# A hybrid encoder layer on one core: operand buffers, copy priority, DMA queues and mixer pacing in the last block

## The chip, the core and the metric

The kernel runs on one core of a Trainium2 chip. The core has five engines that run side by side, each with its own instruction queue in program order: TensorE (PE in the profile, with PEld for its weight loads), VectorE (DVE), ScalarE (ACT), GpSimd (POOL) and SyncE (SP). Data moves between DRAM and the on-chip memory by DMA; a DMA is issued by SP (queue SPq) or by POOL (queue POOLq), and an issue that must wait stands in front of all that was put behind it on the same engine. The metric is the device time of one execution in microseconds (us), lower is better.

## What is computed

One layer of a streaming trunk over 2,064 prompt rows and 64 sample rows of width 1024, in float32:

```python
def _trunk(x, states, segs, p):
    for l in range(DEPTH):                       # DEPTH = 1
        m, ns = _mixer(_rmsnorm(x, p['norm1_w'][l]), l, *st, segs, p)   # input projection, three head groups (SSD, RWKV-7, HGRN2), w_out
        x = x + m
        x = x + _swiglu(_rmsnorm(x, p['norm2_w'][l]), p['w_gate'][l], p['w_up'][l], p['w_down'][l])
    return _rmsnorm(x, p['final_norm_w']), ...

def _swiglu(h, wg, wu, wd):
    return (jax.nn.silu(h @ wg) * (h @ wu)) @ wd
```

The feed-forward width is 2816, that is 22 column blocks of 128. The mixers are causal recurrences in chunks; beside the rows, their final states are returned.

## The kernel before

Each float32 operand of a large product is split into a high and a low part (ACT copies the high part, `AF.Copy` to float32r; DVE, or POOL in the early phase, subtracts for the low one), and a product is three matmuls: high by high, high by low, low by high. A weight block w with both parts is 512 KB; five buffers hold such blocks (WB = 5), and three hold raw 256 KB blocks that are still to be split (tile `raw`, RB = 3).

**The early phase.** Rows are 17 tiles of 128. Nine are worked off in three early blocks of three tiles (class `Ffn`: output projection `out`, gate and up columns and down products in `ffn`, last down products and final norm in `rest`). `early()` runs these blocks as the dense main stream of PE work; the mixers run beside them as side streams ("rw" and "hs", for the RWKV-7 and HGRN2 groups). A planner merges both: each dense step advances a clock `now` by its cost in matmul columns, and a stream may take its next step when its own time, which grows by its step's cost times a scale, is not past `now`. The scales are RWX and HSX (L42): larger scales put more dense work between two steps of a mixer. The last early block does SWITCH of the 22 column blocks of its `ffn` under the planner together with the mixers; then what is left of the mixers is drained, the operands `ya` of the last block (outputs of the mixers) are loaded (24 loads by SP, 256 KB each), and the rest of the `ffn` runs.

**The last block** has the remaining eight tiles and multiplies in blocks of two by two with seven products instead of eight. It runs in this order:

- `first_half(j)`: output projection (key "wo") and norm, which leaves the hidden rows as operands (`op`, `ya`, split at L1412/L1413).
- Pairs i = 0 to 10: gate and up columns, seven products each (`columns`). A bank of sums is copied by ACT from PSUM to a tile `c` (`copy`, L1553). The weight sums t1 to t4 of a pair are made from raw loads (`lraw`, L1534), but for the first PRE = 3 pairs they were made ahead and lie in DRAM (`raw`, L1360). At the end of a pair, `finish` applies the gate (L1604, L1605), forms four sums (L1608 to L1611) and POOL writes the seven results to DRAM (tiles `ma..`, `ms..`, L1614).
- After each pair, `t_sums` makes the sums of two w_down blocks (`wd0` to `wd10`): SP loads four quarters (L1315), DVE adds, POOL stores (L1320).
- The down products (`tokens_first` with key "wd"): seven products, each over 11 k-blocks. Operands come back from DRAM in groups of four k-blocks (`m_group`: load `mraw`, L1638, up to 1 MB; split to `op` by ACT L1412 and DVE L1413). `mraw` has two buffers in a pool l2 that is opened when the pool lp of the pairs is closed and lies in lp's memory. POOL loads the residual rows `acc` (L1656). Results are added to `acc` (L1375).
- `final_norm`: two squares with row sums on ACT (L1133), the sum and the power (L1134, POOL L230), two scalings on DVE (L1138), two 256 KB stores by POOL (L1139).

The order of instructions on each engine is made by a scheduler at build time; memory that is reused makes the new owner wait for the readers and DMAs of the old one.

Of the kernel before, what the change touches and what calls it, by code (L numbers as in the profile page):

```python
# [13 lines left out]
AF = mybir.ActivationFunctionType  # L14
# [5 lines left out]
P = 128  # L20
# [3 lines left out]
NFF = DFF // P  # L24
# [14 lines left out]
GKS = 1  # L39
GLO = 3  # L40
URB = 6
RWX, HSX, HSD = 1.05, 1.0, 6.0  # L42
COL = 1 / 2360
AHEAD = 4
KOUT = [8, 9, 10, 11, 0, 1, 2, 3, 4, 5, 6, 7]
# [1 line left out]
DSTEP = (-1, 2, 6, 9)  # L47
FW = 3
NH = 4
SWITCH = 14  # L50
PRE = 3
TAIL = 4
CW = 384
# [25 lines left out]
def body(tc, A, O, blocks=None, supers=None, dbg=None):  # L79
    nc = tc.nc  # L80
    V, S, G, T = nc.vector, nc.scalar, nc.gpsimd, nc.tensor
# [5 lines left out]
    def pool(st, name, bufs=1, **kw):  # L87
        return st.enter_context(tc.tile_pool(name=name, bufs=bufs, **kw))
# [7 lines left out]
    def mk(p, shape, dt=F32, tag=None, bufs=None):  # L96
        uid[0] += 1
        kw = {} if bufs is None else {"bufs": bufs}
        return p.tile(list(shape), dt, tag=tag, name=f"{tag}_{uid[0]}", **kw)
# [1024 lines left out]
                    nc.sync.dma_start(dbg["y"][k, t], yscr[k][t])  # L1124


    def final_norm(p, xt, t, n, fw):

        s2 = mk(p, [P, 2], tag="s2", bufs=2)
        ss = mk(p, [P, 1], tag="ss", bufs=2)  # L1130
        for hf in range(2):
            dump = mk(p, [P, 512], tag="w2k", bufs=4)
            S.activation(dump[:n], xt[:, hf * 512:hf * 512 + 512], AF.Square, accum_out=s2[:n, hf:hf + 1])  # L1133
        V.tensor_tensor(ss[:n], s2[:n, 0:1], s2[:n, 1:2], ADD)  # L1134
        rs = inv_rms(p, ss, n, 1, 1.0 / D, EPS)
        for hf in range(2):
            cs = slice(hf * 512, hf * 512 + 512)
            V.scalar_tensor_tensor(xt[:, cs], xt[:, cs], rs[:n], fw[:n, cs], MUL, MUL)  # L1138
            G.dma_start(O["y_prompt"][(t - 1) * P:t * P, cs] if t else O["y_sample"][:, cs], xt[:, cs])  # L1139

    class Ffn:

# [132 lines left out]

        def final(self, i, fw):
            t, n = self.tiles[i], self.lens[i]
            final_norm(self.fp, self.acc[:n, i, :], t, n, fw)

    if supers:  # L1280
        stE, st = ExitStack(), ExitStack()
# [3 lines left out]
        def early():  # L1285
            drain(ALLY(EARLY[0]))
            fs[0].start()
            for i, f in enumerate(fs):
# [10 lines left out]
                else:  # L1299
                    yield from f.ffn(0, SWITCH)  # L1300

# [6 lines left out]

        tdram = {}

        def t_sums(key, q):

            def ld(n):
                r = mk(ring, [P, 512], tag="raw", bufs=RB)
                nc.sync.dma_start(r, q[n])  # L1315
                return r

            def st(n, r):
                d = tdram[key, n] = dram.tile([P, 512], F32, tag=f"{key}{n}", name=f"{key}{n}")
                G.dma_start(d, r)  # L1320

            a, b = ld(3), ld(1)
            V.tensor_tensor(a, a, b, SUB)
            st("t3", a)
            c_ = ld(0)
            V.tensor_tensor(b, b, c_, SUB)
            st("t1", b)
            V.tensor_tensor(c_, a, c_, ADD)
            st("t2", c_)
            d_ = ld(2)  # L1330
            V.tensor_tensor(d_, d_, c_, SUB)
            st("t4", d_)

        def quarters(key, kk):
            if key in ("w_gate", "w_up"):
                return [A[key][2 * kk + f][:, h * 512:h * 512 + 512] for h in range(2) for f in range(2)]
            if key == "wo":
                k = kk // 2 * 4 + kk % 2
                return [A["w_out"][d, k + 2 * h] for h in range(2) for d in range(2)]
            return [A["w_down"][(2 * kk + h) * P:(2 * kk + h + 1) * P, d * 512:d * 512 + 512] for h in range(2) for d in range(2)]  # L1340

        def prep_sums():
            for key, kks in (("wo", (4, 5, 0, 1, 2, 3)), ("w_gate", range(PRE)), ("w_up", range(PRE))):
                for kk in kks:
                    t_sums(f"{key}{kk}", quarters(key, kk))
                    yield 35.0

        def parts(raw):
# [62 lines left out]
        def to_parts(hi, lo, src):  # L1411
            S.activation(hi, src, AF.Copy)  # L1412
            V.tensor_tensor(lo, src, hi.bitcast(F32), SUB)  # L1413

        tile_of = lambda h, j: LATE[h][j]
# [23 lines left out]
        acc = [[mk(lo_, [P, D], tag=f"acc{h}{j}", bufs=1) for j in range(NH)] for h in (1, 0)][::-1]  # L1439
# [84 lines left out]
        msc = {(n, g): dram.tile([P, 4, 512], F32, tag=f"m{n}{g}", name=f"m{n}{g}") for n, *_ in PRODS for g in range(3)}  # L1524
        stF = ExitStack()

        def columns(key, i):

            q = dict(zip(("b11", "b12", "b21", "b22"), quarters(key, i)))
            raw = {}  # L1530
            if i >= PRE:
                for n in ("b22", "b12", "b11", "b21"):
                    raw[n] = mk(lp, [P, 512], tag="lraw", bufs=8)
                    nc.sync.dma_start(raw[n], q[n])  # L1534
                b11, b12, b21, b22 = (raw[n] for n in q)
                V.tensor_tensor(b22, b22, b12, SUB)
                V.tensor_tensor(b12, b12, b11, SUB)
                V.tensor_tensor(b11, b22, b11, ADD)
                V.tensor_tensor(b21, b21, b11, SUB)
                raw = {"t3": b22, "t1": b12, "t2": b11, "t4": b21}  # L1540

            def prod(ps, a, b, first=True):
                hi, lo = parts(raw[b]) if b in raw else b_part(key, i, b)
                ah, al = hop[a]
                for k in range(4):
                    wh, wl = (x[:, k * P:(k + 1) * P] for x in (hi, lo))
                    mm(ps, wh, ah[:, k], first and k == 0, False, not first)
                    mm(ps, wh, al[:, k], False, False, not first)
                    mm(ps, wl, ah[:, k], False, k == 3, not first)

            def copy(tag, ps, bufs):
                r = mk(lp, [P, 512], tag=tag, bufs=bufs)
                S.activation(r, ps, AF.Copy)  # L1553
                return r

            add = lambda r, ps: V.tensor_tensor(r, ps, r, ADD)
            pre = i < PRE
            x = xbank()
            prod(x, "s1", "t1")
            c22 = copy("c22", x, 6)  # L1560
            yield
            y = xbank() if pre else ybank()
            prod(y, "a22", "t4")
            c21 = copy("c21", y, 6)
            yield
            z = ybank()
            prod(z, "a11", "b11")
            c11 = copy("c11", z, 4)
            yield
            y = ybank()  # L1570
            prod(y, "a12", "b21")
            add(c11, y)
            yield
            prod(z, "s2", "t2", False)
            c12 = copy("c12", z, 4)
            yield
            if pre:
                add(c12, c22)
                x = xbank()
            prod(x, "s4", "b22", pre)  # L1580
            add(c12, x)
            yield
            prod(z, "s3", "t3", False)
            add(c21, z)
            add(c22, z)
            return c11, c12, c21, c22
# [29 lines left out]
        for j in range(NH):  # L1616
            first_half(j)
        stO.close()
        lp = pool(stF, "lp", reuse_waits="tile")
        pairs = [Pair(i) for i in range(PRE)]  # L1620
        for p_ in pairs:
# [2 lines left out]
        for i in range(NFF // 2):  # L1624
            if i >= PRE:
                pairs.append(Pair(i))
            pairs[i].finish()
            t_sums(f"wd{i}", quarters("wd", i))
        stF.close()


        l2 = pool(st, "l2", reuse_waits="tile")
        mraw = lambda: mk(l2, [P, 4, 512], tag="mraw", bufs=2)

        def m_group(name, kks):
            n = len(kks)
            raw = mraw()
            nc.sync.dma_start(raw[:, :n], msc[name, kks[0] // 4][:, :n])  # L1638
            hi, lo = op_tile()
            to_parts(hi[:, :n], lo[:, :n], raw[:, :n])  # L1640
            return [(hi[:, i], lo[:, i]) for i in range(n)]

        def finish(h, j):
            final_norm(l2, acc[h][j], tile_of(h, j), P, fw)

        def rows_done(a):
            if a == "s1":
                for j in range(NH):
                    finish(1, j)

        acc = [[mk(l2, [P, D], tag=f"acc{h}{j}", bufs=1) for j in range(NH)] for h in range(2)]
        fw = mk(l2, [P, D], tag="nw", bufs=1)
        ahead_ = m_group("a11", range(4))
        for h in range(2):
            for j in range(NH):
                G.dma_start(acc[h][j], xs2[h][j])  # L1656
        G.dma_start(fw, A["fw"].partition_broadcast(P))
        tokens_first("wd", list(range(NFF // 2)), 4, lambda n, kks: ahead_ if (n, kks[0]) == ("a11", 0) else m_group(n, kks), acc, rows_done, lambda prepare: None, lambda j: finish(0, j))
        st.close()
    else:  # L1660
        drain(ALLY(range(last_tile + 1)))
# [110 lines left out]
```

## Time and profile before

| What | Value |
|---|---|
| Three runs | 3590.32, 3579.01, 3581.46 us; median 3581.46 |
| The profiled execution | 3584.01 us; span in the trace 3582.0, so 2.0 lie around it |
| PE busy | 3376.5 us (94%) |
| DVE, ACT, POOL busy | 2200.1 (61%), 1237.6 (35%), 727.5 (20%) |
| Last matmul ends, span ends | 3567.3, 3582.0 us |

PE is the engine with the most work, so time can be saved where PE stands idle, where it runs below its full clock, and behind its last matmul. In the views quoted below a row of the timeline is: start, duration, engine, line, operation, out<-in, shapes, count, and in brackets the idle time before it with what ended that time. A row of the windows is: window, its length, then busy time and count for PE, PEld, DVE, ACT and POOL, the granted TensorE clock (1.00 is full), the share of the DMA engines' time that was busy, and GB/s. A row of the waits is: what waited, for what, total us, times, the longest.

### The profile page before, as it was taken

The numbers are of one execution on the slowest core, as the hardware profiler recorded it, in microseconds if no ns is written. First come the engines' busy times: TensorE is split into PE (matmuls) and PEld (weight loads), VectorE is DVE, ScalarE is ACT, GpSimd is POOL, SyncE is SP. The second block draws the span as 40 slices with busy tenths as digits, with TensorE's granted clock in tenths as the row PEclk, the third lists the DMA queues.
The fourth block names the chain that finished last, engine by engine and source line by source line (L and its number), as shares of the span: only waits on it lengthen the run. The fifth ranks groups of instructions, "written<-read, shape, count | busy, mean of one in ns | idle before, by whom it ended". The sixth has DMA issues, their size and how long they took to land.

```text
span 3582.0 us, 60919 instructions
## 1 busy us (share of the span) xinstructions
PE 3376.5 (94%) x22588; PEld 2950.8 (82%) x22588; DVE 2200.1 (61%) x4940; ACT 1237.6 (35%) x2618; POOL 727.5 (20%) x1022
## 2 busy tenths in 40 slices
PE   7999999999999998889898999999999989999798
PEld 7998789889799996778776899879888868788686
DVE  3358455557766676787777776767425655654453
ACT  4445333344343444344342222223102442223241
POOL 3325202102111112344442211110101002210001
PEclk9999999999999999899999999999999989999899
DMA  9776865555765668788899997676787458865755
GB/s 321 233 224 220 285 213 177 155 161 177 242 218 175 202 195 290 270 282 307 306 309 328 312 330 253 226 266 229 229 276 263 158 162 282 282 217 174 274 180 207
DMA packets 430497, 860.40 MB, mean 240 GB/s; under 512 B 112096, under 2 KB 211944, under 8 KB 426360
## 3 DMA queue, kind: packets, MB, share of 16 engines
q1 hardware_dynamic: 405752, 775.23, 65.7%
q0 software_dynamic: 24448, 81.28, 6.1%
q8 instruction: 178, 2.92, 0.3%
q14 instruction: 119, 0.97, 0.1%
HBM read 603.81 MB, written 252.54 MB: 239 GB/s over the span
## 4 chain that ended last, share of the span: by engine, by line
PE 29%; issue 13%; DMA 6%; DVE 5%; POOL 3%; ACT 1%; SPq 1%; POOLq 0%; DVEq 0%; ACTq 0%
PE g L111 21%; PE d L111 4%; DMA w<-w 2%; PE h L111 2%; PE c L111 1%; DMA raw<-in_w_down 1%; DMA raw<-in_w_gate 1%; POOL w L222 1%; DMA raw<-in_w_up 1%; POOL ms L1614 1%; POOL ma L1614 0%; DMA raw<-in_w_out 0%; DVE acc L1274 0%; DVE tp L640 0%; DVE Xp L641 0%
## 5 line engine op out<-in xcount | busy, mean ns | idle before, releaser
L111 PE MATMUL g<-hhi,w 128*128 128x384 f32 (+3 forms) x3312 | 832.7, 329 | 15.0 <-ACT stage L368 4.7
L111 PEld LDWEIGHTS g<-hhi,w 128*128 128x128 f32 (+1 forms) x3312 | 579.2, 188 | 30.2 <-ACT stage L368 5.1
L111 PE MATMUL g<-h2hi,w 128*128 128x384 f32 (+1 forms) x2112 | 544.4, 334 | 12.6 <-ACT w L220 5.3
L111 PE MATMUL g<-hlo,w 128*128 128x384 f32 (+3 forms) x1680 | 549.1, 327 | 0.0
L111 PEld LDWEIGHTS g<-h2hi,w 128*128 128x128 f32 x2112 | 375.9, 190 | 23.3 <-ACT w L220 7.9
L111 PE MATMUL g<-h2lo,w 128*128 128x384 f32 (+1 forms) x1056 | 349.6, 331 | 0.8 <-DVE h2lo L255 0.8
L111 PEld LDWEIGHTS g<-hlo,w 128*128 128x128 f32 (+1 forms) x1680 | 313.5, 187 | 5.6
L222 POOL TENSOR_TENSOR w<-raw,w 128x512 fp32r<-128x512 f32 x180 | 247.7, 1378 | 336.9 <-ACT w L220 284.4
L111 PE MATMUL g<-w,mhi 128*128 128x512 f32 x792 | 264.3, 411 | 18.3 <-ACT w L220 6.1
L220 ACT ACTIVATE w<-raw 128x512 fp32r<-128x512 f32 x240 | 149.8, 629 | 197.8 <-PE g L111 52.6
L111 PE MATMUL g<-w,op 128*128 128x512 f32 x816 | 197.0, 401 | 22.1 <-ACT op L1412 22.1
L111 PEld LDWEIGHTS g<-w,op 128*128 128x128 f32 x816 | 155.5, 191 | 61.1 <-ACT op L1412 23.0
L111 PEld LDWEIGHTS g<-h2lo,w 128*128 128x128 f32 x1056 | 200.1, 189 | 4.1 <-DVE h2lo L255 1.4
L111 PEld LDWEIGHTS g<-w,mhi 128*128 128x128 f32 x792 | 150.0, 194 | 54.4 <-ACT w L220 7.0
L111 PE MATMUL g<-w,hhi 128*128 128x512 f32 (+1 forms) x544 | 179.8, 411 | 11.4 <-DMA w<-w 7.4
L111 PE MATMUL d<-op,w 128*128 128x512 f32 x720 | 170.4, 395 | 8.2 <-DMA w<-w 8.2
L111 PEld LDWEIGHTS d<-op,w 128*128 128x128 f32 x720 | 136.0, 189 | 39.7 <-issue 9.8
L1274 DVE TENSOR_TENSOR acc<-g,acc 128x512 f32<-128x512 f32 (+1 forms) x198 | 133.0, 684 | 52.1 <-PE g L111 51.8
L640 DVE TENSOR_TENSOR tp<-Xp,b4k 128x60 f32<-128x60 f32 (+24 forms) x527 | 126.1, 239 | 62.8 <-DMA b4k<-psc 50.4
L111 PE MATMUL g<-w,mlo 128*128 128x512 f32 x396 | 159.8, 404 | 0.0
L111 PE MATMUL d<-w,op 128*128 128x512 f32 x612 | 144.1, 395 | 0.0
L111 PEld LDWEIGHTS d<-w,op 128*128 128x128 f32 x612 | 114.7, 187 | 28.1
(435 smaller groups left out, 6214.8 us busy)
## 6 DMA issues: line engine op xcount, KB each, us to landing
w<-w SPq DMA_DIRECT2D x893, 512.0 KB, 4.4
raw<-in_w_down SPq DMA_DIRECT2D x88, 256.0 KB, 4.2
hin<-hg SPq DMA_DIRECT2D x16, 1280.0 KB, 6.0
rin<-rw SPq DMA_DIRECT2D x16, 896.0 KB, 6.0
raw<-in_w_gate SPq DMA_DIRECT2D x56, 256.0 KB, 4.4
raw<-in_w_up SPq DMA_DIRECT2D x56, 256.0 KB, 4.8
hg<-stage SPq DMA_DIRECT2D x64, 192.0 KB, 3.0
raw<-in_w_out SPq DMA_DIRECT2D x48, 256.0 KB, 5.1
```

The costliest lines, as they stand in the source:

```text
L111: return T.matmul(out, lhsT, rhs, start=start, stop=stop, skip_group_check=more)
L220: S.activation(hi, raw, AF.Copy)
L222: (G if units[0] % 4 < GLO else V).tensor_tensor(lo, raw, wt[:, 0], SUB)
L640: V.tensor_tensor(tv, _bc(Xp[:, 0:m, q], 2, w), _bc(Up[:, q, q + 1:32], 1, m), MUL)
L1274: V.tensor_tensor(self.acc[:n, i, cs], ps[:n], self.acc[:n, i, cs], ADD)
L1614: G.dma_start(msc[n, g][:, k, :], r)
```

## The change

Six edits:

1. The loads of gated rows (`m_group`) get a pool of their own, `lm`, opened before the pairs on the other side of the memory, with three buffers of two k-blocks instead of two buffers of four; a group is loaded and split in two halves. The first group is asked for ahead of the `acc` tiles.
2. Copies of a bank in `columns` get high priority in the scheduler for the first three pairs.
3. The loads of `t_sums` go through a queue that the caller names: POOL's for the w_down sums, SP's as before for the sums made ahead.
4. RWX 1.05 to 1.08, HSX 1.0 to 1.03, SWITCH 14 to 18.
5. `final_norm` can take a tile in which the first square's sum already lies; for the first half of the last block's rows these squares are issued after the product "a12", the last that adds to the first 512 columns.
6. The stores of these rows go through SP's queue.

```diff
-RWX, HSX, HSD = 1.05, 1.0, 6.0
+RWX, HSX, HSD = 1.08, 1.03, 6.0
-SWITCH = 14
+SWITCH = 18
...
+    def squares(p, xt, n, hf, s2):
+        dump = mk(p, [P, 512], tag="w2k", bufs=4)
+        S.activation(dump[:n], xt[:, hf * 512:hf * 512 + 512], AF.Square, accum_out=s2[:n, hf:hf + 1])
+
+    def final_norm(p, xt, t, n, fw, queue, s2=None):
...
-        for hf in range(2):
-            dump = mk(p, [P, 512], tag="w2k", bufs=4)
-            S.activation(dump[:n], xt[:, hf * 512:hf * 512 + 512], AF.Square, accum_out=s2[:n, hf:hf + 1])
+        if s2 is None:
+            s2 = mk(p, [P, 2], tag="s2", bufs=2)
+            squares(p, xt, n, 0, s2)
+        squares(p, xt, n, 1, s2)
...
-            G.dma_start(O["y_prompt"][(t - 1) * P:t * P, cs] if t else O["y_sample"][:, cs], xt[:, cs])
+            queue.dma_start(O["y_prompt"][(t - 1) * P:t * P, cs] if t else O["y_sample"][:, cs], xt[:, cs])
...
-        def t_sums(key, q):
+        def t_sums(key, q, queue):
...
-                nc.sync.dma_start(r, q[n])
+                queue.dma_start(r, q[n])
...
-                S.activation(r, ps, AF.Copy)
+                with tc.high_priority() if i < PRE else ExitStack():
+                    S.activation(r, ps, AF.Copy)
...
+        lm = pool(st, "lm", side="right", reuse_waits="tile")
         lp = pool(stF, "lp", reuse_waits="tile")
...
-            t_sums(f"wd{i}", quarters("wd", i))
+            t_sums(f"wd{i}", quarters("wd", i), G)
...
-        mraw = lambda: mk(l2, [P, 4, 512], tag="mraw", bufs=2)
...
-            raw = mraw()
-            nc.sync.dma_start(raw[:, :n], msc[name, kks[0] // 4][:, :n])
             hi, lo = op_tile()
-            to_parts(hi[:, :n], lo[:, :n], raw[:, :n])
+            for a in range(0, n, 2):
+                w = min(2, n - a)
+                raw = mk(lm, [P, 2, 512], tag="mraw", bufs=3)
+                nc.sync.dma_start(raw[:, :w], msc[name, kks[0] // 4][:, a:a + w])
+                to_parts(hi[:, a:a + w], lo[:, a:a + w], raw[:, :w])
...
+        ahead_ = m_group("a11", range(4))
+        sq = [mk(l2, [P, 2], tag="sq", bufs=NH) for _ in range(NH)]
 
         def rows_done(a):
-            if a == "s1":
-                for j in range(NH):
-                    finish(1, j)
+            for j in range(NH):
+                if a == "s1":
+                    final_norm(l2, acc[1][j], tile_of(1, j), P, fw, G)
+                elif a == "a12":
+                    squares(l2, acc[0][j], P, 0, sq[j])
...
+                     lambda j: final_norm(l2, acc[0][j], tile_of(0, j), P, fw, nc.sync, sq[j]))
```

How this moves instructions is shown at three places. The first is SP's queue where the pairs end and the down products begin. Before, `w125` to `w173` are the first five w_down blocks that need no sums, and the first loads of gated rows (`mraw<-ma110`, four k-blocks each) stand behind them:

```order
L216 DMA w_4848_33511<-w230_20537 128x1024
L216 DMA w_4849_33526<-w232_20587 128x1024
L216 DMA w_4871_33645<-w125_16970 128x1024
L216 DMA w_4872_33659<-w137_17385 128x1024
L216 DMA w_4873_33673<-w149_17719 128x1024
L216 DMA w_4874_33687<-w161_18198 128x1024
L216 DMA w_4877_33706<-w173_18600 128x1024
L1638 DMA mraw_4865_33627<-ma110_30194 128x2048
L1638 DMA mraw_4875_33701<-ma111_30195 128x2048
```

In the change, the same stretch of SP's queue:

```order
L216 DMA w_4848_33514<-w230_20381 128x1024
L216 DMA w_4849_33529<-w232_20482 128x1024
L1645 DMA mraw_4889_33782<-ma112_30196 128x512
L1645 DMA mraw_4898_33837<-ms30_30197 128x1024
L216 DMA w_4876_33656<-w125_16884 128x1024
L216 DMA w_4877_33670<-w137_17262 128x1024
L1645 DMA mraw_4899_33841<-ms30_30197 128x1024
L1645 DMA mraw_4909_33914<-ms31_30198 128x1024
L216 DMA w_4878_33684<-w149_17639 128x1024
L216 DMA w_4879_33698<-w161_18022 128x1024
```

The loads of `ma110`, and of the first half of `ma111`, no longer stand here at all: they went up into the pairs. Its last group (`ma112`, which holds pair 10) and the first group of the next product (`ms30`) now stand ahead of `w125`.

The second place is SP's queue around pairs 2 to 4 (`w134`, `w136` belong to pair 2, `w141` to pair 3). Before, loads for the w_down sums (`raw<-in_w_down`) stand between the loads of gate columns (`lraw`) and of weight blocks:

```order
L216 DMA w_4511_31130<-w136_17334 128x1024
L1315 DMA raw_4517_31204<-in_w_down 128x512
L1315 DMA raw_4518_31209<-in_w_down 128x512
L1534 DMA lraw_4562_31521<-in_w_gate 128x512
L1315 DMA raw_4519_31217<-in_w_down 128x512
L1534 DMA lraw_4563_31523<-in_w_gate 128x512
L1315 DMA raw_4558_31501<-in_w_down 128x512
L1534 DMA lraw_4564_31525<-in_w_gate 128x512
L1315 DMA raw_4559_31503<-in_w_down 128x512
L1315 DMA raw_4560_31508<-in_w_down 128x512
L1534 DMA lraw_4565_31527<-in_w_gate 128x512
L216 DMA w_4541_31319<-w141_17491 128x1024
```

In the change SP has only the loads that PE's own work needs, but for one load of gated rows a little later (`ma110`, pairs 2 and 3):

```order
L216 DMA w_4511_31133<-w136_17231 128x1024
L1538 DMA lraw_4562_31524<-in_w_gate 128x512
L1538 DMA lraw_4563_31526<-in_w_gate 128x512
L1538 DMA lraw_4564_31528<-in_w_gate 128x512
L1538 DMA lraw_4565_31530<-in_w_gate 128x512
L216 DMA w_4541_31322<-w141_17416 128x1024
```

```order
L1538 DMA lraw_4572_31560<-in_w_up 128x512
L1645 DMA mraw_4858_33626<-ma110_30194 128x1024
L1538 DMA lraw_4604_31823<-in_w_gate 128x512
L1538 DMA lraw_4605_31825<-in_w_gate 128x512
L1538 DMA lraw_4606_31827<-in_w_gate 128x512
```

The loads that are gone from here stand in POOL's queue now, between the stores of the same sums and the writes of the pairs' results (`wd3`, `wd4` are the sums of two w_down blocks, `ma110` is a result of pair 3):

```order
L1324 DMA wd3t4_31522<-raw_4561_31519 128x512
L1319 DMA raw_4601_31805<-in_w_down 128x512
L1319 DMA raw_4602_31810<-in_w_down 128x512
L1619 DMA ma110_30194<-c11_4542_31336 128x512
L1324 DMA wd4t3_31808<-raw_4600_31803 128x512
L1324 DMA wd4t1_31813<-raw_4601_31805 128x512
L1324 DMA wd4t2_31816<-raw_4602_31810 128x512
L1319 DMA raw_4603_31818<-in_w_down 128x512
```

The third place is ACT's queue where `first_half` ends and the pairs begin: the last splits of hidden rows (`op<-hraw`) and the first four copies of banks. Before:

```order
L1412 ACTIVATE op_4369_30193<-hraw0_4220_29260 128x4x128
L1412 ACTIVATE op_4367_30191<-hraw1_4221_29261 128x4x128
L1412 ACTIVATE op_4369_30193<-hraw0_4220_29260 128x4x128
L1553 ACTIVATE c22_4391_30355<-g_4388_30337 128x512
L1553 ACTIVATE c22_4395_30375<-g_4392_30357 128x512
L1553 ACTIVATE c21_4399_30395<-g_4396_30377 128x512
L1553 ACTIVATE c21_4403_30415<-g_4400_30397 128x512
```

In the change:

```order
L1416 ACTIVATE op_4369_30193<-hraw0_4220_29260 128x4x128
L1416 ACTIVATE op_4367_30191<-hraw1_4221_29261 128x4x128
L1416 ACTIVATE op_4369_30193<-hraw0_4220_29260 128x4x128
L1558 ACTIVATE c22_4391_30358<-g_4388_30340 128x512
L1558 ACTIVATE c21_4399_30398<-g_4396_30380 128x512
L1558 ACTIVATE c22_4395_30378<-g_4392_30360 128x512
L1558 ACTIVATE c21_4403_30418<-g_4400_30400 128x512
```

The copies stand behind the last split as before; the second and third of them have changed places.

More of the change, by code (lines that the diff above doesn't have):

```diff
@@ L1124, in body @@
                     nc.sync.dma_start(dbg["y"][k, t], yscr[k][t])
-    def final_norm(p, xt, t, n, fw):
-        s2 = mk(p, [P, 2], tag="s2", bufs=2)
+    def squares(p, xt, n, hf, s2):
+        dump = mk(p, [P, 512], tag="w2k", bufs=4)
+        S.activation(dump[:n], xt[:, hf * 512:hf * 512 + 512], AF.Square, accum_out=s2[:n, hf:hf + 1])
+    def final_norm(p, xt, t, n, fw, queue, s2=None):
         ss = mk(p, [P, 1], tag="ss", bufs=2)
-        for hf in range(2):
-            dump = mk(p, [P, 512], tag="w2k", bufs=4)
-            S.activation(dump[:n], xt[:, hf * 512:hf * 512 + 512], AF.Square, accum_out=s2[:n, hf:hf + 1])
+        if s2 is None:
+            s2 = mk(p, [P, 2], tag="s2", bufs=2)
+            squares(p, xt, n, 0, s2)
+        squares(p, xt, n, 1, s2)
         V.tensor_tensor(ss[:n], s2[:n, 0:1], s2[:n, 1:2], ADD)
@@ L1277, in final @@
             t, n = self.tiles[i], self.lens[i]
-            final_norm(self.fp, self.acc[:n, i, :], t, n, fw)
+            final_norm(self.fp, self.acc[:n, i, :], t, n, fw, G)
     if supers:
@@ L1344, in prep_sums @@
                 for kk in kks:
-                    t_sums(f"{key}{kk}", quarters(key, kk))
+                    t_sums(f"{key}{kk}", quarters(key, kk), nc.sync)
                     yield 35.0
@@ L1627, in body @@
             pairs[i].finish()
-            t_sums(f"wd{i}", quarters("wd", i))
+            t_sums(f"wd{i}", quarters("wd", i), G)
         stF.close()
         l2 = pool(st, "l2", reuse_waits="tile")
-        mraw = lambda: mk(l2, [P, 4, 512], tag="mraw", bufs=2)
         def m_group(name, kks):
             n = len(kks)
-            raw = mraw()
-            nc.sync.dma_start(raw[:, :n], msc[name, kks[0] // 4][:, :n])
             hi, lo = op_tile()
-            to_parts(hi[:, :n], lo[:, :n], raw[:, :n])
+            for a in range(0, n, 2):
[3 more added lines that the diff above has]
+                to_parts(hi[:, a:a + w], lo[:, a:a + w], raw[:, :w])
             return [(hi[:, i], lo[:, i]) for i in range(n)]
-        def finish(h, j):
-            final_norm(l2, acc[h][j], tile_of(h, j), P, fw)
+        ahead_ = m_group("a11", range(4))
+        sq = [mk(l2, [P, 2], tag="sq", bufs=NH) for _ in range(NH)]
         def rows_done(a):
-            if a == "s1":
-                for j in range(NH):
-                    finish(1, j)
+            for j in range(NH):
[3 more added lines that the diff above has]
+                    squares(l2, acc[0][j], P, 0, sq[j])
         acc = [[mk(l2, [P, D], tag=f"acc{h}{j}", bufs=1) for j in range(NH)] for h in range(2)]
         fw = mk(l2, [P, D], tag="nw", bufs=1)
-        ahead_ = m_group("a11", range(4))
         for h in range(2):
@@ L1657, in body @@
         G.dma_start(fw, A["fw"].partition_broadcast(P))
-        tokens_first("wd", list(range(NFF // 2)), 4, lambda n, kks: ahead_ if (n, kks[0]) == ("a11", 0) else m_group(n, kks), acc, rows_done, lambda prepare: None, lambda j: finish(0, j))
+        tokens_first("wd", list(range(NFF // 2)), 4, lambda n, kks: ahead_ if (n, kks[0]) == ("a11", 0) else m_group(n, kks), acc, rows_done, lambda prepare: None,
+                     lambda j: final_norm(l2, acc[0][j], tile_of(0, j), P, fw, nc.sync, sq[j]))
         st.close()
```

## The prediction

> **What bounds the kernel now.** I read the page's busy shares first, then the windows over the stretches that the change touches, then the timeline of PE, SP, ACT and POOL at the gaps.
>
> ```profile
> PE 3376.5 (94%) x22588; PEld 2950.8 (82%) x22588; DVE 2200.1 (61%) x4940; ACT 1237.6 (35%) x2618; POOL 727.5 (20%) x1022
> ```
> ```profile
> 3006.00:3176.00 170.00, 158.46 (x673) 127.87 (x672) 101.86 (x164) 45.60 (x80) 33.07 (x61) 0.98 0.80 274
> 3176.00:3330.00 154.00, 153.89 (x673) 125.93 (x671) 75.93 (x120) 46.42 (x78) 15.72 (x29) 1.00 0.55 181
> 3330.00:3350.00 20.00, 1.11 (x3) 0.92 (x4) 6.04 (x9) 1.91 (x1) 7.43 (x14) 0.60 0.90 320
> 3350.00:3400.00 50.00, 50.00 (x207) 39.99 (x206) 25.19 (x22) 18.99 (x18) 0.00 (x0) 0.95 0.76 287
> 2586.00:2612.00 26.00, 17.36 (x64) 12.63 (x63) 5.81 (x9) 1.02 (x2) 0.00 (x0) 0.87 1.14 331
> 1200.00:2000.00 800.00, 725.37 (x5558) 626.26 (x5557) 588.02 (x1352) 324.84 (x721) 271.36 (x258) 0.95 0.82 279
> 2000.00:2400.00 400.00, 395.34 (x2898) 347.70 (x2897) 277.51 (x684) 97.98 (x237) 57.18 (x76) 1.00 0.81 278
> ```
>
> PE is the bound; what can be won lies where it idles. 3006 to 3176 and 3176 to 3330 hold the same 673 matmuls, four pairs each, yet the first takes 16 us more. 3330 to 3350 is a hole between the pairs and the down products. 1200 to 2000, where mixers run beside dense work, has 74.6 us of PE idle, against 4.7 in the 400 us after it.
>
> **The hole at 3330.**
>
> ```profile
> 3324.23 5.66 PE L111 MATMUL d<-ya,w 128*128 128x512 f32 x24
> 3348.89 28.01 PE L111 MATMUL g<-w,op 128*128 128x512 f32 x108 [19.00 <-ACT op L1412]
> ```
> ```profile
> 3337.34 14.17 SPq L1638 DMA_DIRECT2D mraw<-ma  x3
> ```
> ```profile
> 3346.93 1.91 ACT L1412 ACTIVATE op<-mraw 128x2048 fp32r<-128x2048 f32 x1 [17.80 <-DMA mraw<-ma]
> ```
> ```profile
> 3315.70 0.54 POOL L1614 DMA_DIRECT2D ma<-c  x1 [18.36 <-DVE c L1605]
> ...
> 3334.04 1.75 POOL L1614 DMA_DIRECT2D ms<-c  x3 [0.18 <-issue]
> 3335.78 2.11 POOL L1656 DMA_DIRECT2D acc<-xs  x4
> ```
>
> PE waits 19.0 us for the split of the first gated group, the split waits for its load, and the load is issued at 3337.34, after the last stores from the pairs' memory (3334.04 plus 1.75 and a landing), because its buffer lies there. With buffers of its own that wait has no cause: by SP's order pairs 0 to 3 are loaded during the pairs, and ACT and DVE split them in the last pair. Late now is `w125`. It stands behind the load of `ma112`, which needs POOL's store of 3315.70 (the median landing of such a store is the 3.8 us of the row below); so it is issued near 3320 to 3321 and, at 4.3 us, lands before 3326, ahead of the 3329.9 where the pairs end.
>
> ```profile
> w<-w SPq DMA_DIRECT2D x71, 512.0 KB, 4.3
> ...
> ma<-c POOLq DMA_DIRECT2D x32, 256.0 KB, 3.8
> ```
>
> The next blocks stand behind two more operand loads, which wait for splits of about 1 us each (1.91 for twice the size), and are needed 2.8 us apart; five buffers cover that. So the 19.0 go. So does the slow start: 108 matmuls took 28.01 us, while the later groups show 2.96 for 12 with 0.15 of overhang, 2.81, so 25.2 for 108; 2.8 more, at a granted clock of 0.60 and 0.95.
>
> ```profile
> 3377.20 2.96 PE L111 MATMUL g<-w,op 128*128 128x512 f32 x12
> 3380.01 2.03 PE L111 MATMUL d<-w,op 128*128 128x512 f32 x8
> ```
>
> The Trainium skill, page "TensorE: Matmul & The Clock Gate", section on the HAM clock gate, says that one idle window of about 3.4 us halves the clock and a busy one restores it; an estimate from it is 1.7 us lost instead of 2.8, and the sum would be 1.1 us smaller. The granted clock agrees in kind, and the measured 2.8 is used.
>
> What can come back: the `acc` loads, 4.5 MB with the norm weights, now move while PE wants weights. The nearest row against me is 2586 to 2612, where the 6 MB of `ya` loads meet weight loads and PE idles 8.6 us; 4.5/6 of it is 6.5. For me speaks that from 3350 on PE was busy 50.00 of 50.00 with 287 GB/s. I take 2. **Term: -19.0 - 2.8 + 2.0 = -19.8, bounds -21.8 and -13.**
>
> **The loads of the w_down sums.**
>
> ```profile
> SPq L1534 <- DVE w L1352: 47.7, 22, 6.6
> SPq L1315 <- DMA wd8t<-raw: 12.7, 4, 6.4
> SPq L1315 <- DMA wd4t<-raw: 8.7, 3, 5.3
> SPq L1315 <- DMA wd3t<-raw: 7.8, 2, 7.1
> ```
> ```profile
> PE d L111 <- DMA w<-w: 11.5, 6, 3.5
> ```
> ```profile
> raw<-in_w_down SPq DMA_DIRECT2D x33, 256.0 KB, 4.5
> ```
> ```profile
> 3059.88 7.36 PE L111 MATMUL d<-ya,w 128*128 128x512 f32 x24 [2.77 <-DMA w<-w]
> ...
> 3114.47 10.09 PE L111 MATMUL d<-op,w 128*128 128x512 f32 x36 [3.52 <-DMA w<-w]
> ```
>
> In 3006 to 3176 SP stands again and again at L1315, until a store of an earlier sum has landed and freed one of three raw buffers. The weight blocks are behind it, and PE waits for them six times, 11.5 us, plus the slow stretches after the longer gaps (7.36 for 24 matmuls that take 5.66 elsewhere). From 3176, with these loads gone, PE has no gap. On POOL the same waits stand before stores of results and of other sums, which nobody needs before the down products, but for the two loads of gated rows that SP now issues early (`ma110` of pairs 2 and 3, `ma111` of pairs 4 and 5). POOL is busy 33 of 170 us; the 33 loads in this stretch add 0.54 us each, 18 us. The store that the first of these loads waits for lands about 4 us after the pair's gate, just when SP would issue the next `lraw`; I leave 3 us for that. **Term: -16 + 3 = -13, bounds -16 and -3** (at both places POOL is late by 6.4, the longest wait for one store: +12.8).
>
> The Trainium skill, page "DMA: Bandwidth & Descriptors", section "Issuing engines are not separate DMA queues", says that DMAs of all issuing engines share the same sixteen engines, and that issuing from several saves only the issuing time. By that rule this term is nothing and the sum -26.6; it is the second rival below.
>
> **Bank copies.** PE's longest gap in the last block beside the hole ends with these copies:
>
> ```profile
> 2897.83 0.63 ACT L1412 ACTIVATE op<-hraw 128x512 fp32r<-128x512 f32 x1 [1.17 <-DVE hraw L1515]
> 2898.37 2.04 ACT L1553 ACTIVATE c<-g 128x512 f32<-128x512 f32 x4
> ```
> ```profile
> 2899.00 6.23 PE L111 MATMUL g<-ya,w 128*128 128x512 f32 x16 [10.04 <-ACT c L1553]
> ```
>
> In the new order they still stand behind the last split of hidden rows; two of them trade places. The split waits for DVE as before. **Term: 0, bounds -10 and 0.**
>
> **The end.**
>
> ```profile
> 3567.34 0.69 DVE L1375 TENSOR_TENSOR acc<-g,acc 128x512 f32<-128x512 f32 x1 [0.26 <-PE g L111]
> 3567.95 2.73 DVE L1138 SCALAR_TENSOR_TENSOR acc<-acc,rs,nw 128x512 f32<-128x512 f32 x4
> 3570.59 0.15 DVE L1134 TENSOR_TENSOR ss<-s 128x1 f32<-128x1 f32 x1
> ```
> ```profile
> 3573.18 1.21 POOL L1139 DMA_DIRECT2D out_y_prompt<-acc  x2 [1.08 <-DVE acc L1138]
> ```
> ```profile
> DMA to landing us min/median/max: 2.4/6.0/8.6
> ```
>
> The last tile's sum waits not for squares but for four scalings of the tiles before it. In the change two of them move ahead, but the remaining two wait for a power that starts after the last addition, so I count 0.3. Landing: 6.0 us is the median of POOL's stores, 4.5 that of SP's loads of the same size in the row above: 1.5, if a store through SP lands like a load. **Term: -1.8, bounds -5 and 0.**
>
> **Mixer pacing.** Scales 3% larger put 3% more dense work between two mixer steps, and four more column blocks of the last early `ffn` lie under it.
>
> ```profile
> PE g L111 <- ACT w L220: 13.5, 6, 5.6
> PE h L111 <- ACT us L920: 9.0, 4, 3.9
> PE h L111 <- DVE hin L832: 8.2, 6, 2.4
> ```
>
> In 1200 to 2000 PE waits in turn for split weights and for mixer results. No row has the new order, so the bounds are wide: a quarter of the 74.6 us goes (-20, towards the 2000 to 2400 row), or a fifth of it comes on top (+15). Thinner mixers point to less waiting, but 3% is little and every chain meets other work: **-5**. The `ya` loads meet weight loads as before: 0.
>
> **Sum:** -19.8 - 13 - 0 - 1.8 - 5 = -39.6 against the profiled 3584.0 (2.0 of it outside the span, taken as unchanged) gives 3544.4. That execution is 2.5 above the median of the three runs (3581.5); I go a little down for it: 3543.
>
> **Rivals.**
>
> 1. The reordered mixers make PE wait more (+15 instead of -5): 3563. For it: DVE is busy 588 of 800 us there, POOL 271. Against: the mixers come in thinner.
> 2. The engines' load, not SP's order, makes the waits in pairs 3 to 6, so moving loads wins nothing: 3584.0 - 26.6 = 3557. For it: DMA share 0.80 and 274 GB/s there, against 0.55 and 181 where PE never waits. Against: 0.81 and 278 in 2000 to 2400 with 4.7 us of idle, and SP's waits name the stores.
> 3. The copies do come earlier on the chip: another -10, 3533. Against: ACT's order.
> 4. Slower: the mixers' order goes wrong as a whole. PE takes matmuls in order, so a mixer step placed ahead of its operands holds up dense work behind it; place 1200 to 2000, price the idle there. If it doubles, 3543 + 5 + 74.6 = 3623. The kernel becomes slower by 0.3% (3592) from 54 us of added idle on. Against: the side streams' dense cover grows and does not shrink.
>
> **How the numbers follow.** Forecast 0.60 (3528 with the mixers alone at their good bound, 3550 and 3553 with the hole or the sums alone at their poor one), rival 1 0.13, rival 2 0.15, rival 3 0.05, rival 4 0.07. The range takes in the forecast, rivals 1, 2 and 3 with some us about them, and leaves out rival 4 and the outer parts of the others: 3518 to 3568. A difference of 0.3%, 10.7 us, is about what a measurement of this kernel can tell from none. Faster (below 3570.7): forecast, rivals 2 and 3, and 0.08 of rival 1: 0.88. Same: the rest of rival 1 and 0.02 of rival 4, 0.07. Slower: the rest of rival 4, 0.05.
>
> **What would show it.** Hole: `g<-w,op` follows the last `d<-ya,w` within 2 us, at a clock near 1.00; a gap with DMA w<-w as its end would show the collision. Sums: 3006 to 3176's 673 matmuls in 154 to 158 us, no SP wait at the moved line; rival 2 keeps 11 us of PE waits on w<-w with SP free. Copies: the 10 us gap ended by ACT c stays. End: the span ends about 12 us after the last matmul, not 14.7. Mixers: idle of 1200 to 2000 near 70. The forecast is wrong if that idle moves by more than 20, or if the gap at 3330 stays above 8.

## The result, and the profile after

| | Before | After |
|---|---|---|
| Median, four runs each on one chip | 3583.79 us (3579.01 to 3590.32) | 3550.24 us (3539.10 to 3554.66) |
| Ratio after to before | | 0.9900, 95% interval 0.9872 to 0.9929 |
| The profiled execution, its span | 3584.01, 3582.0 us | 3539.10, 3537.3 us |

The changed kernel is 33.5 us faster, 7 us less than forecast and inside the range. The profiled execution of the change is the fastest of its four, so the span's difference (44.7 us) is larger than the medians'. A second profile of the same kernel, from the experiments below, stands beside it. Cut at the same instructions (`g<-w,op` is the first product of the last block, `g<-ya,w` the first of the pairs):

| Stretch, us | Before | After | After, second profile |
|---|---|---|---|
| Span's start to the last block | 2743.7 | 2729.5 | 2737.0 |
| Output projection and norm, `first_half` | 126.7 | 127.0 | 126.8 |
| Pairs | 459.4 | 456.6 | 459.7 |
| Hole behind the pairs | 19.0 | 0 | 0 |
| Down products | 218.4 | 215.8 | 215.8 |
| Last matmul to span's end | 14.7 | 8.6 | 8.7 |
| Span | 3582.0 | 3537.3 | 3547.6 |

The page of the profile after, busy time of each engine:

```profile
PE 3367.3 (95%) x22588; PEld 2940.6 (83%) x22588; DVE 2216.0 (63%) x4961; ACT 1227.5 (35%) x2635; POOL 745.9 (21%) x1058
```

PE's busy time is 9 us less for the same 22588 matmuls (3376.5 before); the other 36 us are idle time that is gone. PE's timeline where the pairs end:

```profile
3307.43 5.66 PE L111 MATMUL d<-ya,w 128*128 128x512 f32 x24
3312.92 28.16 PE L111 MATMUL g<-w,op 128*128 128x512 f32 x120
```

The 19.00 us are gone to the last tenth: the first down product starts as the last pair ends, and 120 matmuls take 28.16 where 108 took 28.01. The windows of the same kernel over the four pairs, the place of the hole, the mixers and the early phase:

```profile
2989.80:3159.90 170.10, 160.56 (x687) 129.27 (x686) 97.89 (x157) 43.77 (x79) 49.26 (x91) 0.99 0.79 273
3310.00:3345.00 35.00, 35.00 (x152) 28.12 (x151) 14.36 (x19) 7.98 (x11) 7.57 (x15) 1.00 1.02 390
1200.00:2000.00 800.00, 731.14 (x5506) 629.77 (x5500) 608.69 (x1357) 322.18 (x715) 267.80 (x261) 0.96 0.83 284
0.00:800.00 800.00, 761.90 (x5470) 696.00 (x5471) 446.79 (x1134) 323.29 (x716) 193.99 (x341) 0.99 0.70 224
```

The second row shows the `acc` loads beside the first down products: 390 GB/s, and PE busy 35.00 of 35.00 at full clock. The first row holds pairs 3 to 6 and a few matmuls of pair 7: 687 matmuls in 170 us, 673 before. Counted off PE's timeline by 168 matmuls a pair, pairs 3 to 6 take 167.0 us (165.3 in the second profile) against 170.1 before, where 154 to 158 were forecast. The waits of SP and of PE from 2990 to 3180:

```profile
SPq L1538 <- DVE w L1356: 137.7, 31, 12.0
SPq L1645 <- DMA ma<-c: 5.0, 1, 5.0
```
```profile
PE d L111 <- DMA w<-w: 5.0, 3, 2.0
PE d L111 <- DVE w L1356: 4.9, 4, 2.1
```

No row names the moved line any more, and SP now waits at its own `lraw` loads for DVE instead (137.7 us; 47.7 before, in a window 20 us shorter): L1356 makes the low part of a gate or up sum, and is the last to read an `lraw` buffer. PE still waits: 5.0 us for blocks and 4.9 for these low parts (11.2 with two smaller rows), where before it was 11.5 for blocks.

### The profile page after: what moved, and what is told of

It is laid out like the page before. It is cut to its first block, busy times and chain, and to the rows that moved or that the text cites. A ratio compares the mean times of both kernels' runs of the same rounds, so it can differ in the third digit from the quotient of the medians.

```text
span 3537.3 us, 61018 instructions
## 1 busy us (share of the span) xinstructions
PE 3367.3 (95%) x22588; PEld 2940.6 (83%) x22588; DVE 2216.0 (63%) x4961; ACT 1227.5 (35%) x2635; POOL 745.9 (21%) x1058
## 4 chain that ended last, share of the span: by engine, by line
PE 64%; DMA 13%; DVE 11%; issue 6%; POOL 2%; ACT 2%; SPq 2%; POOLq 0%; DVEq 0%; ACTq 0%
PE g L111 46%; PE d L111 8%; PE c L111 4%; PE h L111 3%; DMA w<-w 3%; DMA raw<-in_w_down 2%; DVE tp L640 1%; DVE Xp L641 1%; DMA hin<-hg 1%; DMA raw<-in_w_up 1%; POOL w L222 1%; DMA hg<-stage 1%; DVE gcv L418 1%; DMA dec<-cu 1%; DVE acc L1278 0%
## 5 line engine op out<-in xcount | busy, mean ns | idle before, releaser
L111 PEld LDWEIGHTS d<-op,w 128*128 128x128 f32 x720 | 135.0, 188 | 33.5 <-DVE w L1356 4.1
L640 DVE TENSOR_TENSOR tp<-Xp,b4k 128x60 f32<-128x60 f32 (+24 forms) x527 | 126.8, 241 | 51.2 <-DMA b4k<-psc 38.3
```

Of the source, the lines that this page charges most:

```text
L111: return T.matmul(out, lhsT, rhs, start=start, stop=stop, skip_group_check=more)
L640: V.tensor_tensor(tv, _bc(Xp[:, 0:m, q], 2, w), _bc(Up[:, q, q + 1:32], 1, m), MUL)
```

## The experiments

A ratio is to the kernel before on the same chip, with its 95% interval. The median of before was 3588.65, 3582.48 and 3589.34 us on the three chips used.

### The parts alone

Four kernels are the kernel before with one part each. Edit 1:

```diff
+        lm = pool(st, "lm", side="right", reuse_waits="tile")
...
-            raw = mraw()
-            nc.sync.dma_start(raw[:, :n], msc[name, kks[0] // 4][:, :n])
+                raw = mk(lm, [P, 2, 512], tag="mraw", bufs=3)
+                nc.sync.dma_start(raw[:, :w], msc[name, kks[0] // 4][:, a:a + w])
```

> The kernel before with edit 1 alone (own buffers for the gated rows, halves of two k-blocks). Theory A (the hole of 19.0 us and the slow start behind it go, and the weight loads are not hurt): the matmuls of the first down product follow those of the last pair without a gap, 12 of them in 2.8 us from the start, the time is about 21 to 22 us shorter than before, and the pairs' waits for w stay near 11 us. Rival (the early loads in SP's queue hold up weight loads in the pairs, or the acc loads collide with them): the hole goes, but PE gaps on DMA w<-w grow elsewhere and the time is 8 to 16 us shorter.

Edit 3:

```diff
-            t_sums(f"wd{i}", quarters("wd", i))
+            t_sums(f"wd{i}", quarters("wd", i), G)
```

> The kernel before with edit 3 alone (loads of the w_down sums through POOL's queue). Theory B (the block moves from SP to DVE: DVE's adds for the sums wait for their loads in DVE's order, and behind them stand the low parts of weights and the release of the lraw buffers): pairs 3 to 6 still take 165 to 171 us instead of 154, SP waits for DVE at the lraw line, the time is within 4 us of before. Rival (SP was the only block, and in the changed kernel it was the gated rows' early loads that gave the gain back): the four pairs take 154 to 158 us and the time is 11 to 16 us shorter.

Edit 4:

```diff
-RWX, HSX, HSD = 1.05, 1.0, 6.0
+RWX, HSX, HSD = 1.08, 1.03, 6.0
-SWITCH = 14
+SWITCH = 18
```

> The kernel before with edit 4 alone (RWX 1.08, HSX 1.03, SWITCH 18). Theory C (thinner mixers make PE wait less): the first matmul of the last block (g<-w,op) comes about 14 us earlier, as in the changed kernel, and the time is 10 to 15 us shorter. Rival (the 14 us between the two profiles are mostly chance between executions): the time is within 5 us of before.

Edits 5 and 6:

```diff
+                elif a == "a12":
+                    squares(l2, acc[0][j], P, 0, sq[j])
...
-            G.dma_start(O["y_prompt"][(t - 1) * P:t * P, cs] if t else O["y_sample"][:, cs], xt[:, cs])
+            queue.dma_start(O["y_prompt"][(t - 1) * P:t * P, cs] if t else O["y_sample"][:, cs], xt[:, cs])
```

> The kernel before with edits 5 and 6 alone (early first squares, stores of the last rows through SP). Theory D (the landing of the last store sets the end): from the last matmul to the end of the span 8 to 9 us instead of 14.7, the time 5 to 6 us shorter. Rival (the order of DVE sets it): 12 to 13 us, the time 1 to 2 us shorter.

| Part alone | Median, us | Ratio | In us |
|---|---|---|---|
| Edit 1, gated rows | 3574.51 | 0.9958 (0.9945 to 0.9971) | -14.1 |
| Edit 3, sums by POOL | 3588.60 | 0.9999 (0.9986 to 1.0012) | 0 |
| Edit 4, mixers | 3582.87 | 0.9982 (0.9971 to 0.9993) | -5.8 |
| Edits 5 and 6, end | 3587.48 | 0.9995 (0.9980 to 1.0010) | -1.2 |

Together they make -21, and the whole change makes -29 (its second lot of runs, below) to -33.5: some 10 us come only from parts together. Edit 2, the copies' priority, was not run alone; the gap that it aims at stays at 10.03 us. In the profile of edit 1 the hole is gone, down products take 215.8, and PE is full where the loads meet; but the pairs take 4.5 us more than before, and the gain of 14.1 us lies in the rival's range. PE's waits in the pairs of that kernel:

```profile
PE d L111 <- DMA w<-w: 14.9, 7, 3.1
```

Before it is 11.5 us, and the early loads of gated rows stand between the weight loads on SP. With edit 3 alone PE's longest row for blocks falls to 7.7 us, but waits for low parts come (13.9 us with all rows), pairs 3 to 6 take 174.8 us, and SP stands just as long for DVE:

```profile
SPq L1534 <- DVE w L1352: 135.5, 31, 13.0
```
```profile
PE d L111 <- DMA w<-w: 7.7, 3, 3.7
```

So moving the loads away from SP moved the wait and won nothing by itself. The Trainium skill, page "DMA: Bandwidth & Descriptors", section "Issuing engines are not separate DMA queues", would have it so, and this run agrees (0.9999). Beside the early loads of gated rows it does not: there the same move is worth some 8 to 10 us (edit 3 undone, below), and the measurement decides.

Edit 4 alone brings the last block 3 us earlier (2740.5 against 2743.7), not 14, and its 5.8 us lie between theory and rival. Edits 5 and 6 alone leave 10.9 us from the last matmul to the end of the span, also between theory (8 to 9) and rival (12 to 13).

### Is it DVE's order?

The waits now name DVE. One reading: an add of a w_down sum that waits for its load holds up what stands behind it in DVE's order, the adds and low parts of the gate and up columns. The four adds of these sums go to POOL:

```diff
-            V.tensor_tensor(a, a, b, SUB)
+            eng.tensor_tensor(a, a, b, SUB)
...
-            t_sums(f"wd{i}", quarters("wd", i), G)
+            t_sums(f"wd{i}", quarters("wd", i), G, G)
```

> The changed kernel with the four additions of each w_down sum on POOL instead of DVE, so that the waits for their loads and the additions leave DVE's order too. Theory B (in the changed kernel these additions hold up DVE, and with it weights' low parts and the lraw buffers): PE waits for neither DVE w nor DMA w in pairs 3 to 6, each takes 38.5 to 39.5 us, and the time is 12 to 16 us shorter than the changed kernel's. Rival (the load on the DMA engines makes the waits, whoever stands in line): the pairs take 40 to 45 us as before and the time is within 4 us of the changed kernel's.

Beside it the changed kernel once more:

> The changed kernel once more, unchanged, in more executions and with another profile. Theory E (executions of one kernel differ by some 10 us, and the changed kernel's first profile is a quick one): median 3548 to 3556; in the profile the first matmul of the last block comes later than the 2729.5 of the first profile, by 5 to 12 us; the hole stays at 0 and the down products at 215.8. Rival (the first profile is typical): 2729 to 2731, time near 3540.

Pair 0's first step written ahead of the third tile of `first_half`, so that its bank copies no longer stand behind the last splits (its `c22` copies get a pool of two buffers of their own for that, and the other pairs have four instead of six):

```diff
+            if j == 2:
+                pairs[0].step()
...
-            p_.step()
+            if p_.i:
+                p_.step()
```

> The changed kernel with the first step of pair 0 written ahead of the third first_half and its two copies in buffers of their own (c22 then has four buffers), so that these two copies really stand earlier on ACT. Theory F (the 10 us gap at the start of the pairs is the copies' place behind the last splits): the gap falls from 10 to about 5 us or less, since two of four banks come free in time for 5.5 us of products; the time is 4 to 6 us shorter than the changed kernel's. Rival (DVE, which works without pause there, sets the pace): the same idle time shows up at DVE w or split hidden rows, and the time is within 2 us.

And both:

> The changed kernel with both: additions of the w_down sums on POOL, and pair 0's first copies earlier. If theories B and F hold: 16 to 22 us shorter than the changed kernel. If their rivals hold: within 5 us of it.

| Kernel | Median, us | Ratio |
|---|---|---|
| Changed, again | 3553.20 | 0.9916 (0.9898 to 0.9934) |
| Adds on POOL | 3555.89 | 0.9923 (0.9900 to 0.9946) |
| Copies earlier | 3544.53 | 0.9895 (0.9876 to 0.9914) |
| Both | 3549.16 | 0.9905 (0.9886 to 0.9924) |

The changed kernel's second profile starts its last block 7.5 us later than the first, as theory E has it.

The reading about DVE falls: with the adds on POOL the time is 2.7 us from the changed kernel's, and PE waits as long. The slow pairs come one pair later in this profile, which is the slowest execution of its six; windows and PE's waits over pairs 4 to 7:

```profile
3054.00:3227.00 173.00, 161.16 (x674) 129.85 (x673) 104.72 (x135) 47.00 (x82) 80.16 (x108) 0.96 0.75 256
```
```profile
PE d L111 <- DMA w<-w: 8.5, 4, 4.9
PE d L111 <- DVE w L1356: 3.3, 1, 3.3
```

Pairs 3 to 7 together take 211.4 us, against 207.8 and 209.0 in the changed kernel's two profiles. The kernel with both, 4.0 us shorter than the changed one, lies where the rivals put it.

The earlier copies cut the gap ahead of the pairs from 10.03 to 7.45 us. PE's timeline of the changed kernel and of this one:

```profile
2883.74 6.44 PE L111 MATMUL g<-ya,w 128*128 128x512 f32 x20 [10.03 <-ACT c L1558]
```
```profile
2897.38 2.93 PE L111 MATMUL g<-op,w 128*128 128x512 f32 x6 [7.45 <-ACT c L1558]
```

That is 2.6 us, and two waits of 0.7 and 0.6 us ahead of the gap are gone as well; theory F had the gap at 5 or less. The medians differ by 8.7 with intervals that overlap, so the rest is not shown.

### Is it the volume of loads beside a pair?

The w_down sums need 44 loads, four for each of eleven sets, and most of them gather in the first pairs, since little holds them back but their buffers: 31 fall into pairs 3 to 6 of the changed kernel. In two kernels an addition of POOL that reads a product of a pair stands ahead of each load, so that one set of sums goes with each pair. In the first, set i waits for pair i:

```diff
+                if hold is not None:
+                    G.tensor_tensor(r[:, :1], hold[:, :1], hold[:, :1], ADD)
...
-            t_sums(f"wd{i}", quarters("wd", i), G)
+            t_sums(f"wd{i}", quarters("wd", i), G, held)
```

> The changed kernel with the w_down sums bound to their pairs: a one-column addition on POOL reads a result of pair i into each raw buffer ahead of the load for wd i, so that one set of sums is made per pair, over all eleven pairs, and no more than that runs beside pairs 3 to 6. Theory G (it is the traffic: loads of weights land in 7 us instead of 4 where two or three sets of sums run beside a pair, and the loop of lraw buffers then misses its time): weights land in 4 to 5.5 us in pairs 3 to 6, the pairs' excess over 38.46 us falls from 16 to 20 us in all to below 8, and the time is 6 to 14 us shorter than the changed kernel's. Rival (any set beside a pair costs its 2 us or so, spread or not): the excess is as large in sum, now over pairs 3 to 10, and the time is within 4 us.

The changed kernel with edit 3 undone:

```diff
-            t_sums(f"wd{i}", quarters("wd", i), G)
+            t_sums(f"wd{i}", quarters("wd", i), nc.sync)
```

> The changed kernel with edit 3 undone: the w_down sums' loads through SP again. Theories B and G as they stand (the queue does not matter): pairs 3 to 6 take 165 to 175 us, the time is within 4 us of the changed kernel's. Rival (edit 3 does help beside the early gated rows): 6 to 15 us longer than the changed kernel.

And the copies written earlier, with set i bound to the pair before:

```diff
+            prev, held = held, pairs[i].finish()
+            t_sums(f"wd{i}", quarters("wd", i), G, prev)
```

> The changed kernel with pair 0's first copies earlier (as tried) and the sums bound to the pair before (wd i after pair i - 1). If theory G holds: 10 to 18 us shorter than the changed kernel; if not, 3 to 8 us shorter, from the copies alone.

| Kernel | Median, us | Ratio | Pairs in the profile, us |
|---|---|---|---|
| Set i with pair i | 3584.38 | 0.9985 (0.9972 to 0.9999) | 472.8 |
| Edit 3 undone | 3567.74 | 0.9943 (0.9925 to 0.9961) | 469.3 |
| Set i with pair i-1, copies earlier | 3538.01 (3537.28 to 3540.27) | 0.9863 (0.9843 to 0.9882) | 442.8 |

The last one is faster than both kernels. Its windows over pairs 3 to 6, its waits and its row of the DMA issues in this stretch:

```profile
2998.00:3157.00 159.00, 156.16 (x675) 127.33 (x674) 89.84 (x143) 45.18 (x80) 34.89 (x76) 0.99 0.71 239
```
```profile
PE g L111 <- DMA w<-w: 2.1, 1, 2.1
PE d L111 <- DMA w<-w: 0.8, 1, 0.8
```
```profile
raw<-in_w_down POOLq DMA_DIRECT2D x16, 256.0 KB, 6.9
```

The changed kernel has 31 of these loads in its stretch:

```profile
raw<-in_w_down POOLq DMA_DIRECT2D x31, 256.0 KB, 5.2
```

With half the sums' loads in these pairs the engines move 239 GB/s instead of 273, PE waits 3 us instead of 10, and pairs 3 to 6 take 158.8 us instead of 167.0. The earlier copies are not the reason. With them alone these pairs take 170 us, and with set i bound to pair i, without them, 159 (the copies alone first):

```profile
2998.90:3169.20 170.30, 159.43 (x674) 127.77 (x674) 96.57 (x156) 42.50 (x78) 49.22 (x91) 0.98 0.78 271
```
```profile
3025.00:3183.70 158.70, 155.90 (x673) 127.22 (x672) 88.10 (x140) 45.06 (x80) 34.99 (x75) 0.99 0.71 238
```

So it is shown that the sets crowded into these pairs cause the waits, by their loads or by the stores and adds that go with them; with one set beside each, pairs 3 to 10 of the fastest kernel lose 5 us in all, nearly all of it in pair 5. By which path is not shown, and two are unlikely: SP stands as long for DVE in the fastest kernel (121.4 us of 159, against 126.8 of 170), and three of its four pairs run in 38.4 to 38.5 us, without loss, though weight blocks land hardly sooner. The expectation had a weight block land in 4 to 5.5 us; its median fell only from 7.0 to 6.6 and its longest from 9.1 to 7.2.

```profile
DMA to landing us min/median/max: 4.8/7.0/9.1
```
```profile
DMA to landing us min/median/max: 3.7/6.6/7.2
```

The first is the changed kernel's, the second the fastest one's. By the ratios this kernel is 13 to 19 us faster than the changed one, 10 to 18 expected.

With set i bound to its own pair the kernel is some 25 us slower than the changed one, not 6 to 14 faster: the binding was a new wait. The `raw` buffers are shared with SP's loads of ready sums, and SP stood 19.4 us for a store that came late (SP's waits from 2930 to 3010); PE then stood twice for a split (PE's timeline):

```profile
SPq L1366 <- DMA wd1t<-raw: 19.4, 1, 19.4
```
```profile
2965.90 7.78 PE L111 MATMUL d<-op,w 128*128 128x512 f32 x24 [11.76 <-ACT w L1357]
...
3005.99 4.64 PE L111 MATMUL d<-op,w 128*128 128x512 f32 x10 [10.34 <-ACT w L1357]
```

The last sums came behind the pairs too, and the down products took 229.3 us instead of 215.8. Pairs 1 and 2 took 52.5 and 51.5 us; pairs 3 to 10 took 38.4 to 39.0 each but for one of 42.8, which speaks for the crowding as well.

With edit 3 undone the changed kernel loses 8 to 10 us against its second run (ratios 0.9943 and 0.9916, whose intervals just overlap). PE's waits in the pairs of the two, edit 3 undone first:

```profile
PE d L111 <- DMA w<-w: 16.0, 7, 3.7
...
PE d L111 <- DVE w L1356: 2.2, 1, 2.2
```
```profile
PE d L111 <- DVE w L1356: 5.4, 6, 1.7
PE d L111 <- DMA w<-w: 4.2, 2, 2.4
```

That is 18.2 against 9.6, the same 8 to 9 us. So edit 3 wins nothing beside the old loads of gated rows and, as far as two intervals that just overlap can show it, 8 to 10 us beside the early ones; this is most of what the parts alone lacked.

## Why the prediction held, and where it did not

The time held; one of its five terms did not, and another was much too small. That the sum came within 7 us owes something to luck: the sums' term was 10 us or more too large, and the hole, the end and the mixers together 7 us too small. The terms against what the runs showed:

| Term | Forecast, us | Shown, us |
|---|---|---|
| Hole and clock | -19.8 | -21.6 (-19.0 and -2.6) |
| Loads of the w_down sums | -13 | 0 to -3 in the pairs |
| Bank copies | 0 | 0 (10.04 and 10.03) |
| End | -1.8 | -6.1 |
| Mixers | -5 | -5.8 |
| Sum | -39.6 | -33.5 |

**The hole.** Right in mechanism and size. The 2 us left for the collision of the `acc` loads did not come (35.00 of 35.00); the clock was 1.00, and 120 matmuls in 28.16 us are 25.3 for 108, where 25.2 was forecast. (The slow start before was 2.6 us and not 2.8: the forecast took the overhang off the 12 matmuls and not off the 108.) Not foreseen was what the early loads of gated rows cost in the pairs: 3.4 us more waiting for blocks with edit 1 alone. The forecast charged them only through POOL's lateness.

**The sums.** This is the step that failed: "On POOL the same waits stand before stores of results and of other sums, which nobody needs before the down products." The waits of SP at the moved line did vanish, and those of PE did not (11.5 us before, 11.2 after); pairs 3 to 6 got 3 to 5 us shorter and not 13. The forecast took SP's order for the cause and read the waits of PE off as gain. Rival 2 had the pairs right as to edit 3: alone it gave 0.9999, and DMA share and GB/s of these pairs stayed at 0.79 and 273 (0.80 and 274 before). What rival 2 did not have is that the move pays once gated rows are loaded early. Its counter-argument in the forecast, that 2000 to 2400 moves as much with almost no idle, still stands: the bytes moved are not the whole, and what in the pairs makes PE so short of blocks is open.

**The copies.** As forecast. That they stand behind the last split is the cause at least in part: written earlier, 7.45 us of the 10.03 are left. Rival 3 did not come.

**The end.** Mis-sized, and outside the bound of -5. From the last matmul to the end of the last scaling it is 5.33 us against 6.24. Timeline of DVE and of SP's queue after:

```profile
3528.72 0.69 DVE L1379 TENSOR_TENSOR acc<-g,acc 128x512 f32<-128x512 f32 x1
...
3532.60 1.41 DVE L1142 SCALAR_TENSOR_TENSOR acc<-acc,rs,nw 128x512 f32<-128x512 f32 x2 [0.73 <-POOL rs L230]
```
```profile
3533.38 0.99 SPq L1143 DMA_DIRECT2D out_y_prompt<-acc  x2
```

So -0.9 (0.3 forecast). The stores of these last tiles land in 2.5 and 2.0 us:

```profile
out_y_prompt<-acc POOLq DMA_DIRECT2D x6, 256.0 KB, 2.5
```
```profile
out_y_prompt<-acc SPq DMA_DIRECT2D x8, 256.0 KB, 2.0
```

The forecast's 6.0 is the median of all 32 such stores of the kernel; the 24 earlier ones land in 6.5, these last ones much sooner. The rest is shown by the strip of DMA activity, 40 slices, before from 3568 to 3582 and after from 3525 to 3537:

```profile
DMA  0000009959799990009959500000000000000000
```
```profile
DMA  0000006999901999940000299993002999930000
```

A slice is 0.35 us before and 0.30 after, so the last data moved until 3576.1 and 3535.8. From the last scaling to there it is 2.5 and 1.8 us: -0.7, where 1.5 was forecast. Behind the last data the span still lasts 5.9 us before and 1.5 after. These 4.4 us had no term, and they are not the work of edits 5 and 6 alone: from the last matmul to the end it is 10.9 us with these two, 10.8 with edit 3 alone, and 8.6 with all.

**The mixers.** The size was right. Timed alone -5.8 (interval -10.4 to -2.5); from the span's start to the last block four profiles with the old pacing took 2745.4 us on average, nine with the new 2739.7. The place was half right: idle time fell from 74.6 to 68.9 us in 1200 to 2000, and in 0 to 800 PE is busy 10 us more. Edit 4 alone, then edit 1 alone, which has the old pacing:

```profile
0.00:800.00 800.00, 760.30 (x5468) 695.18 (x5469) 444.43 (x1134) 322.45 (x716) 193.73 (x341) 0.99 0.70 224
```
```profile
0.00:800.00 800.00, 751.42 (x5310) 685.96 (x5311) 434.60 (x1126) 324.68 (x713) 197.46 (x341) 0.98 0.69 222
```

Part of that is given back behind it. The forecast's 54 us of added idle for a slower kernel should be 44 (3548 and 44 make 3592); nothing else hangs on it. Rivals 1 and 4, with mixers that make PE wait more, did not come.

By their shown sizes the terms make -21.6 - 5.8 - 6.1 = -33.5 with the pairs at 0, which is the medians' difference; so close a fit is partly luck, since executions of one kernel lie 20 us apart and more.

## What to carry to other kernels

When a wait goes because a load is moved to another queue, ask whether the loads themselves become fewer in that stretch: here moving them gave nothing alone, and halving them in the same pairs cut PE's waits from 10 to 3 us. Spread prefetches over the steps, and look which buffers they share with urgent loads: bound to the result of the same pair they stood in such a buffer and cost 25 us, bound to that of the pair before they won 13 or more (with the copies earlier). A stage that waits for operands of memory it takes over is repaired by buffers of its own, and its own gain can be read off the trace almost to the microsecond (21.8 forecast without the collision, 21.6 shown), but not what its loads cost elsewhere (14.1 alone).

## What the runs showed of the hardware

- The span goes on after the last data has moved (read from the same strips, to a slice of about 0.4 us), by a time that goes with the queues used: 5.9 us with sums by SP and last stores by POOL (before), 4.0 with both by SP (edits 5 and 6 alone; 3.9 with edit 3 undone), 2.2 with both by POOL (edit 3 alone), 1.5 with sums by POOL and last stores by SP (after). What it is was not tried.
- One kernel's executions spread far more than the forecast had in mind: 29 runs of before on one chip lay from 3579.4 to 3599.7 us, 12 of the changed kernel with edit 3 undone from 3554.9 to 3584.6. The kernel with the sums' loads spread over the pairs lay within 3 us in four runs; whether that is more than chance stays open.
- After the hole TensorE's granted clock stays at half for a while that differs between kernels with the same hole (windows of 1 us from the first matmul on): 5.7 us before, 5.8 with edit 3 alone, 5.3 with edit 4 alone, 3.9 with edits 5 and 6 alone, behind holes of 18.6 to 19.0 us.
